# Strassen pairs of a two-layer mixer: weight sums, evacuations and attention spread over fixed steps

## The chip, the cores and the metric

The kernel runs on one core of a Trainium2 chip. The metric is the time of one execution on the device in microseconds (us). A core has five engines that run side by side, each with its own in-order queue: TensorE (PE, matmuls; its weight loads are listed as PEld), VectorE (DVE), ScalarE (ACT), GpSimd (POOL) and SyncE (SP, which here only issues DMAs). They wait for one another and for DMAs through semaphores. An instruction that waits holds up everything behind it on its engine. DMAs are moved by 16 DMA engines; SP and POOL each have a queue to them.

## The reference, cut to what matters

Two layers over a sequence of 1024 rows of 1024 numbers in float32:

```
h = rmsnorm(x, norm_g[l]) * (1 + scale) + shift        # scale, shift, gate from c
p = h @ w_in[l]                                         # 1024 x 1024 by 1024 x 9224
mq, mk, mv, mo, mz, mi, mf, rq, rk, rv, rz = split_cols(p)
y_m = sigmoid(mo) * layernorm(mlstm(silu(conv(mq, mk)), mv, mi, mf)) * silu(mz)     # 4 heads of 256
y_r = layernorm(retention(rotary(rq, rk), rv)) * silu(rz)                           # 4 heads of 256
x = x + gate * (concat(y_m, y_r) @ w_out[l])
```

A final rmsnorm follows. The mLSTM and retention cells are chunkwise attention with a carried state.

## The kernel before, in words

All matrix products are in float32 by three passes: an operand is split into a high part (rounded to fp32r) and a low part (the rest), and `mm3` (L153 to L156) adds high x high, high x low and low x high. A split is a ScalarE cast for the high part and a subtraction on POOL or VectorE for the low part (`split_to`, L758 to L760).

The input projection is the bulk. Two column blocks of weights and the two halves of the sequence form a 2 x 2 block problem, done with seven products in place of eight (a Strassen form, `ORDER` L598). The seven right sides (F, `build_forms` L570) are sums of blocks of the normalised input, made once a layer. The seven left sides are sums of four weight blocks, made anew for each pair by `weight_forms` (L601). Blocks of weights come as 128 x 512 tiles of 256 KB. For one set of seven, `weight_forms` loads three raw tiles on SP's queue (L607), lets POOL issue three accumulating DMAs onto them (L623, L632, L633), makes one sum on VectorE (L627), splits five tiles, and gets the other two sides without a raw tile (`loaded`, L615): POOL's DMA brings the tile straight into the high part (L617), ScalarE writes its negative into the low part (L618), and an accumulating DMA adds the tile again (L619).

`pair_units` (L662) runs the seven products of a pair, twelve wide matmuls each, and yields after each. It evacuates after a product: products 0, 2 and 3 are copied out by ScalarE (L674), since the same bank is accumulated further by a later product, and others are combined by VectorE and handed to `done`, which runs the whole chain for that quarter at once: the gate (L542, L547), convolution and SiLU (`conv_silu` L762), or rotary (`rot_done` L834), and then the split and the stores to DRAM (`spill` L809). `vpair_units` (L690) does the same for the values of two heads, with narrow matmuls, two halves to a step; its copies are L720 and its stores L693.

A layer's order is written by hand in `plan` (L1450): z pairs, q and k pairs of each head, v pairs of two heads, and a pairs (z and o together): 30 jobs, 26 pairs of seven steps and 4 v pairs of fourteen, 238 steps. `Feeder` (L649) makes the left sides in the order of use, at most five ahead (AHEAD = 4), from five high, five low and five raw buffers. `run_units` calls `tick` (L133) after each step; `tick` advances the generators that were launched: `attention` of a head (L862) four ticks after its k pair, the condition rows (`ada_rows` L275), the gate chain, the rotary tables. A head's attention loads q, k and v from DRAM, computes scores, values and state updates for four chunks, and normalises (`normalise` L1027; its root is POOL's L1043 or L1047, its scaling ScalarE's L1051, the transposed store L1060).

PE's order is the program's. The order of the other engines is made by the framework's scheduler from the program's order and a simple model of times; instructions inside `tc.high_priority()` (the evacuations) come earlier. Of the output projection (`OutLoads` L1099, `out_units` L1129) and the startup list (L1352) the change touches little.

Of the kernel before, what the change touches and what calls it, by code (L numbers as in the profile page):

```python
# [19 lines left out]
P = 128  # L20
# [16 lines left out]
NB = 61  # L37
NACC = 6
NTH = 4
NW = 5  # L40
NRAW = 5
AHEAD = 4
# [47 lines left out]
def tile_hybrid_trunk(ctx, tc, x, xt, c, positions, w_ada, b_ada, norm_g, w_in, w_blk, w_val, conv_w, conv_b,  # L90
# [38 lines left out]
    def launch(gen, delay=0):  # L129
        uid[0] += 1  # L130
        pending.append([clock[0] + delay, uid[0], gen])

    def tick():  # L133
        clock[0] += 1
        while True:
            due = [p for p in pending if p[0] <= clock[0]]
            if not due:
                return
            p = min(due, key=lambda q: (q[0], q[1]))
            try:  # L140
                p[0] = clock[0] + next(p[2])
            except StopIteration:
                pending.remove(p)

# [8 lines left out]
    def mm3(o, lt, rt, start, stop, more=False):  # L153
# [29 lines left out]
           for l in range(DEPTH)]  # L183
    mdr = [dpool.tile([NH, T], F32, name=f"mdr{l}") for l in range(DEPTH)]
# [90 lines left out]
    def ada_rows(l, c0, accs):  # L275
        acc = wt("acc", 512, NACC)
        accs.append(acc)
        prev = None
        for k in range(KT + 1):
            raw = None  # L280
            if k < KT:
                raw = wt("acc", 512, NACC)
                Q.dma_start(raw, w_ada[l, k * P:(k + 1) * P, c0:c0 + 512])
            if k == 1:
                V.tensor_scalar(acc, prev, cact[:, 0:1], None, ALU.mult)
            elif k > 1:
                V.scalar_tensor_tensor(acc, prev, cact[:, k - 1:k], acc, ALU.mult, ALU.add)
            prev = raw
            yield 2

    def ada_columns_later(l):
        for half in range(2):
            accs = []
            for which in range(2):
                yield from ada_rows(l, which * D + half * 512, accs)
            yield 2
            pt = ps_a()
            for which in range(2):
                for i in range(4):
                    PE.matmul(pt[:, which * 4 + i:which * 4 + i + 1], accs[which][:, i * P:(i + 1) * P], ones,  # L300
                              start=True, stop=True)
            finish_gsh(l, half * 4, 4, pt[:, 0:4], pt[:, 4:8])
            yield 1

    def gate_rows(l, res):
        for half in range(2):
            accs = []
            yield from ada_rows(l, 2 * D + half * 512, accs)
            brow = wt("th", 512, NTH)
# [5 lines left out]
            a2 = (wt("wH", 512, NW, F32R), wt("wL", 512, NW, F32R))  # L315
# [5 lines left out]
            g = bt()  # L321
            V.tensor_copy(g, pt)
            res.append(g)
# [38 lines left out]
    def load_w_raw(l, c0):  # L362
        for p in range(2):
            raw = wt("raw", 512, NRAW)
            Q.dma_start(raw, w_block(l, c0, p))
            yield raw

    def split_w(raw, eng=G, tiles=None):
        wH, wL = tiles or (wt("wH", 512, NW, F32R), wt("wL", 512, NW, F32R))
        split_to((wH, wL), raw, eng)  # L370
        return [(wH[:, a * P:(a + 1) * P], wL[:, a * P:(a + 1) * P]) for a in range(4)]

    def third(pair, p):
        return [t[:, p * 512:(p + 1) * 512] for t in pair]

    def load_w(l, c0):
        res = []
        for raw in load_w_raw(l, c0):
            res += split_w(raw)
        return res  # L380
# [16 lines left out]
    def rotary_tables():  # L397
        c1, c2, c3 = two_pi_split()
        t0, t1 = wt("q", 1024, 2), wt("kc", 1024, 1)
        ang, turn, tmp, rnd = (t0[:, i * CH:(i + 1) * CH] for i in range(4))  # L400
        a1, pos = (t1[:, i * CH:(i + 1) * CH] for i in range(2))
        a2 = ang
        for n in range(4):
            i, cs = n // 2, slice((n % 2) * CH, (n % 2 + 1) * CH)
            Q.dma_start(pos.bitcast(I32), positions[0:1, n * CH:(n + 1) * CH].to_broadcast([P, CH]))
            yield 2
            V.tensor_copy(ang, pos.bitcast(I32))
            V.tensor_scalar(ang, ang, kc[:, C_FREQ:C_FREQ + 1], None, ALU.mult)
# [4 lines left out]
            V.scalar_tensor_tensor(turn, a2, c2, turn, ALU.mult, ALU.add)  # L413
            for src, cc in ((a1, c2), (a2, c1), (a1, c1)):
# [13 lines left out]
            yield 2  # L428
# [113 lines left out]
    def gate_z(src, g, sign=1.0):  # L542
        th = wt("th", 512, NTH)
# [3 lines left out]
    def gate_o(src, g, store, sign=1.0):  # L547
        th = wt("th", 512, NTH)
# [21 lines left out]
    def build_forms(hT):  # L570
        F = {"11": [hT[k][0] for k in range(4)], "21": [hT[k][0] for k in range(4, 8)],
             "22": [hT[k][1] for k in range(4, 8)], "U1": [], "U2": [], "U3": [], "U4": []}
# [11 lines left out]
        for k in range(4):  # L584
# [8 lines left out]
            u4 = whole(hT[k + 4][0])  # L593
            V.scalar_tensor_tensor(u4, u2, -1.0, u4, ALU.mult, ALU.subtract)
            keep("U4", u4)
        return F
# [4 lines left out]
    def weight_forms(blk, first):  # L601
        def tiles():
            return wt("wH", 512, NW, F32R), wt("wL", 512, NW, F32R)

        def raw(src):
            t = wt("raw", 512, NRAW)
            Q.dma_start(t, src)  # L607
            return t

        def split(r, eng):  # L610
            w = tiles()
            split_to(w, r, eng)
            return w

        def loaded(src):  # L615
            w = tiles()
            G.dma_start(w[0], src)  # L617
            A.activation(w[1], f(w[0]), AF.Copy, scale=-1.0)  # L618
            G.dma_start(w[1], src, accum_op=ALU.add)  # L619
            return w  # L620

        a, s1, s3 = raw(blk[0][0]), raw(blk[1][0]), raw(blk[0][0])
        G.dma_start(s1, blk[1][1], accum_op=ALU.add)  # L623
        if first == "21":
            yield loaded(blk[0][1])
        w = split(a, G)
        V.tensor_tensor(a, a, s1, ALU.add)  # L627
        yield w
        if first == "11":
            yield loaded(blk[0][1])  # L630
        w = split(a, V)
        G.dma_start(a, blk[0][1], accum_op=ALU.add)  # L632
        G.dma_start(s3, blk[1][0], accum_op=ALU.add)  # L633
        yield w
        yield split(s1, G)
        yield split(s3, V)
        yield split(a, G)
        yield loaded(blk[1][1])

    def pair_forms(l, cols2):  # L640
        for w in weight_forms([[w_block(l, c, kh) for kh in range(2)] for c in cols2], "11"):
            yield [(w[0][:, k * P:(k + 1) * P], w[1][:, k * P:(k + 1) * P]) for k in range(4)]

    def vpair_forms(l, heads):
        gens = [weight_forms([[w_val[l, h, kh * 2 + kp] for kh in range(2)] for h in heads], "21") for kp in range(2)]
        for ws in zip(*gens):
            yield [(w[0][:, a * HD:(a + 1) * HD], w[1][:, a * HD:(a + 1) * HD]) for w in ws for a in range(2)]

    class Feeder:  # L649
        def __init__(self, gens):  # L650
            self.gens, self.ready = gens, []
            self.forms = (w for g in gens for w in g())

        def take(self):
            while len(self.ready) <= AHEAD:
                w = next(self.forms, None)
                if w is None:
                    break
# [895 lines left out]
```

## Time and profile before

| what | us |
|---|---|
| median of 2 runs (2924.39 to 2930.87) | 2927.63 |
| the profiled execution | 2911.5 |
| its span, first to last instruction | 2909.8 |
| PE busy in the span | 2279.8 |
| VectorE / ScalarE / POOL busy | 1677.8 / 1142.9 / 1151.3 |
| the longest wait of PE in total, for the copies of L674 | 326.0 |

Busy time of PE is the sum of matmuls that overlap, so a share of 78% does not mean that 22% is left; the spacing of their starts tells. A row of groups gives line, engine, operation, tiles written and read, count, then busy time and mean duration in ns, then the idle time of the engine before them with what ended it. The granted clock is that of PE: 1.00 is full speed.

### The profile page before, as it was taken

The page shows a single profiled execution, that of the slowest core. Times are in us where ns is not written, and L with a number is a line of the kernel's source. Part 1 is how long each engine was busy: PE and PEld are TensorE (multiplying, and loading weights), DVE is VectorE, ACT ScalarE, POOL GpSimd, SP SyncE. Part 2 cuts the span into 40 slices and gives each one's busy share as a digit, 9 for nine tenths or more (in the row PEclk, how much of TensorE's full clock was granted, in tenths as well). Part 3 has the DMA queues.
Part 4 walks back from the last instruction along what each step waited for, and adds up shares of the span by engine and source line. Part 5 has one row for each costly group of instructions (what it writes and reads, how often), then busy time and mean ns, then how long its engine had stood idle before and what let it go on. Part 6 is the DMA issues. An engine that isn't in the chain of part 4 may idle for free. (4 is left out here: it accounts for less than half of the span.)

```text
span 2909.8 us, 35824 instructions
## 1 busy us (share of the span) xinstructions
PE 2279.8 (78%) x11483; PEld 1931.8 (66%) x11483; DVE 1677.8 (58%) x3073; ACT 1142.9 (39%) x2091; POOL 1151.3 (40%) x1174
## 2 busy tenths in 40 slices
PE   4878787768777767689998788788777776777998
PEld 3668666657565755577776677667766575666777
DVE  4875365655655556656638556456455556574744
ACT  4523233233434344444354333333344434353433
POOL 0533454444434343422266344255343434343123
PEclk7978898888898888799998898889888888898999
DMA  6277787878777877768542787688777787776766
GB/s 212 52 169 199 180 222 199 228 215 240 203 208 186 225 205 186 196 172 275 199 141 62 184 223 210 175 231 230 211 205 184 190 223 184 193 203 171 237 209 170
DMA packets 532553, 567.91 MB, mean 195 GB/s; under 512 B 196466, under 2 KB 347770, under 8 KB 532364
## 3 DMA queue, kind: packets, MB, share of 16 engines
q1 hardware_dynamic: 463676, 440.55, 48.3%
q0 software_dynamic: 68544, 124.81, 24.0%
q8 instruction: 90, 1.47, 0.2%
q14 instruction: 99, 0.81, 0.1%
q10 hardware_dynamic: 144, 0.26, 0.0%
HBM read 409.20 MB, written 156.27 MB: 194 GB/s over the span
## 5 line engine op out<-in xcount | busy, mean ns | idle before, releaser
L154 PE MATMUL pp<-b,wH 128*128 128x512 f32 x1616 | 681.6, 422 | 338.1 <-ACT acc L674 326.0
L156 PE MATMUL pp<-b,wL 128*128 128x512 f32 x1616 | 664.8, 411 | 13.3 <-DMA wL<-in_w_blk_dram 8.0
L155 PE MATMUL pp<-b,wH 128*128 128x512 f32 x1616 | 668.0, 413 | 4.3 <-DVE b L1120 4.3
L154 PEld LDWEIGHTS pp<-b,wH 128*128 128x128 f32 x1616 | 327.1, 202 | 431.2 <-ACT acc L674 351.2
L760 POOL TENSOR_TENSOR wL<-raw,wH 128x512 fp32r<-128x512 f32 x276 | 392.0, 1433 | 405.4 <-ACT wH L759 332.2
L759 ACT CAST wH<-raw 128x512 fp32r<-128x512 f32 x476 | 289.7, 616 | 372.0 <-PE pp L155 129.8
L156 PEld LDWEIGHTS pp<-b,wL 128*128 128x128 f32 x1616 | 326.3, 202 | 90.2 <-DMA wL<-in_w_blk_dram 9.3
L155 PE MATMUL pp<-wL,b 128*128 128x256 f32 (+1 forms) x1024 | 325.2, 318 | 64.5 <-DMA wL<-in_w_val_dram 57.7
L155 PEld LDWEIGHTS pp<-b,wH 128*128 128x128 f32 x1616 | 328.5, 203 | 70.1 <-DVE b L1120 6.5
L154 PE MATMUL pp<-wH,b 128*128 128x256 f32 (+1 forms) x1024 | 325.7, 318 | 55.4 <-ACT acc L720 24.5
L156 PE MATMUL pp<-wH,b 128*128 128x256 f32 (+1 forms) x1024 | 321.8, 314 | 0.2
L155 PEld LDWEIGHTS pp<-wL,b 128*128 128x128 f32 x1024 | 215.3, 210 | 74.3 <-DMA wL<-in_w_val_dram 61.0
L154 PEld LDWEIGHTS pp<-wH,b 128*128 128x128 f32 x1024 | 215.0, 210 | 66.6 <-ACT acc L720 25.8
L618 ACT ACTIVATE wL<-wH 128x512 fp32r<-128x512 f32 x136 | 85.7, 630 | 430.2 <-DMA wH<-in_w_blk_dram 288.8
L760 POOL TENSOR_TENSOR acc<-acc,acc 128x512 fp32r<-128x512 f32 x128 | 179.7, 1420 | 156.4 <-ACT acc L759 126.0
L619 POOL DMA_DIRECT2D wL<-in_w_blk_dram x104 | 92.0, 884 | 343.1 <-ACT wL L618 260.4
L760 DVE TENSOR_TENSOR wL<-raw,wH 128x512 fp32r<-128x512 f32 x200 | 156.7, 785 | 111.6 <-ACT wH L759 111.1
L156 PEld LDWEIGHTS pp<-wH,b 128*128 128x128 f32 x1024 | 214.9, 210 | 7.3 <-DVE b L1120 2.4
L771 DVE SCALAR_TENSOR_TENSOR acc<-pp,cols,acc 128x511 f32<-128x511 f32 (+2 forms) x192 | 142.4, 742 | 33.4 <-ACT acc L766 32.1
L627 DVE TENSOR_TENSOR raw<-raw,raw 128x512 f32<-128x512 f32 x68 | 54.8, 807 | 147.7 <-POOL wL L760 104.2
L759 ACT CAST acc<-acc 128x512 fp32r<-128x512 f32 x128 | 78.4, 617 | 130.7 <-DVE acc L848 48.3
L760 POOL TENSOR_TENSOR sL<-th,sH 128x384 fp32r<-128x384 f32 (+1 forms) x64 | 62.3, 973 | 108.9 <-ACT sH L759 87.8
(342 smaller groups left out, 4393.1 us busy)
## 6 DMA issues: line engine op xcount, KB each, us to landing
raw<-in_w_blk_dram SPq DMA_DIRECT2D x171, 256.0 KB
raw<-in_w_blk_dram POOLq DMA_DIRECT2D x156, 256.0 KB, 5.3
vdr<-acc SPq DMA_DIRECT2D x128, 256.0 KB
ring<-vdr SPq DMA_DIRECT2D x64, 512.0 KB
qdr<-acc SPq DMA_DIRECT2D x128, 256.0 KB
q<-qdr SPq DMA_DIRECT2D x64, 512.0 KB
kfr<-acc SPq DMA_DIRECT2D x128, 256.0 KB
kc<-kfr SPq DMA_DIRECT2D x64, 512.0 KB
```

The source lines that it names most:

```text
L154: PE.matmul(o, lt[0], rt[0], start=start, stop=False, skip_group_check=more)
L155: PE.matmul(o, lt[0], rt[1], start=False, stop=False, skip_group_check=more)
L156: PE.matmul(o, lt[1], rt[0], start=False, stop=stop, skip_group_check=more)
L618: A.activation(w[1], f(w[0]), AF.Copy, scale=-1.0)
L619: G.dma_start(w[1], src, accum_op=ALU.add)
L627: V.tensor_tensor(a, a, s1, ALU.add)
L759: A.copy(dst[0], src)
L760: eng.tensor_tensor(dst[1], src, f(dst[0]), ALU.subtract)
L771: V.scalar_tensor_tensor(acc[:, d:], pt[:, 0:HALF - d], wcol, acc[:, d:], ALU.mult, ALU.add)
```

## The change

The weight tiles. Raw tiles and low parts share one ring of 13 buffers (R, 128 x 512); high parts keep five. `Feeder` is now a list of events at fixed steps: each load, sum, high part and low part of a set has its lead before the step that uses it, and `step` emits what is due. All seven loads are plain and on SP's queue; the sums S1, S2, S4 and S3 are accumulating DMAs on POOL's queue, of which S2 += S1 and S4 += S2 read a tile in SBUF. `POOL_LOW` says which low parts POOL makes; VectorE makes the other four.

```
+    NAMES = ("a11", "a12", "S2", "S1", "S3", "S4", "a22")
+    VNAMES = ("a12", "a11", "S2", "S1", "S3", "S4", "a22")
+    POOL_LOW = ("a12", "S3", "a22")
...
+    def ring_load(src):
+        r = wt("R", 512, NR)
+        Q.dma_start(r, src)
+        return r
+
+    def high(r, h=None):
+        h = wt("wH", 512, NW, F32R) if h is None else h
+        A.copy(h, r)
+        return h
+
+    def low(h, r, eng=G):
+        lo = wt("R", 512, NR, F32R)
+        eng.tensor_tensor(lo, r, f(h), ALU.subtract)
+        return lo
...
+        def quad(self, names, blk, t0, u):
+            r, h = {}, {}
+            at = {n: t0 + u * i for i, n in enumerate(names)}
+            a11, a12, a21, a22 = blk[0][0], blk[0][1], blk[1][0], blk[1][1]
...
+            def add(n, src):
+                G.dma_start(r[n], r[src] if isinstance(src, str) else src, accum_op=ALU.add)
...
+            T2 = at["S2"]
+            ev(T2 - 10, load, "S1", a21)
+            ev(T2 - 8, load, "S2", a11)
+            ev(T2 - 8, add, "S1", a22)
+            ev(T2 - 6, load, "S4", a12)
+            ev(T2 - 6, add, "S2", "S1")
+            ev(T2 - 4, add, "S4", "S2")
+            T4 = at["S3"]
+            ev(T4 - 7, load, "S3", a21)
+            ev(T4 - 5, add, "S3", a11)
+            for n, src in (("a11", a11), ("a12", a12), ("a22", a22)):
+                ev(at[n] - 7 + u, load, n, src)
+            for n in names:
+                ev(at[n] - 4 + u, hi, n)
+                ev(at[n] - 2, lo, n, G if n in POOL_LOW else V)
+            return r, h
```

The evacuations. The chains of `done` become generators that are launched and give out one link a step: the convolution (scaling, three shifted sums, tanh, product, transposed copy and split, stores), the gates, the rotary parts, and the stores of the values.

```
+    def conv_chain(l, hg, which, m, half, pt, halo):
...
+        yield 1
         for d in range(1, 4):
...
+        yield 1
+        th = wt("acc", 512, NACC)
         A.activation(th, acc, AF.Tanh, scale=0.5)
+        yield 1
         V.scalar_tensor_tensor(acc, th, 1.0, acc, ALU.add, ALU.mult)
-        return acc
+        yield 1
+        yield from spill(acc, l, hg, which, m, half)
...
+        A.copy(hi, src)
+        G.tensor_tensor(lo, src, f(hi), ALU.subtract)
+        yield 1
+        for o, t in late:
+            Q.dma_start(o, t)
         Q.dma_start(dst[m], f(hi))
         Q.dma_start(dst[2 + m], src)
```

Attention follows a table of 43 steps, one entry a step; `scores` and `update` are generators of three links, the sums of the values and `normalise` are launched a step later, and loading and splitting of the transposed k are apart ("t" and "s"). A lock lets the next head begin when the one before has reached step 23; a head's attention is launched 6 steps after its k pair, in place of 4.

```
+    TABLE = ("q0 k0 v0 d0 d1 t0", "", "", "m0", "s0 S0", "k1", "m1 q1", "v1", "V001", "S1 t1", "U01",
+             "k2 q2 d2", "s1 v2", "V10 U2 m2", "S2", "k3 d3", "V11 U3", "t2 q3", "s2 v3", "", "V20 U4 m3", "S3", "",
+             "V21 U5", "", "", "", "V30", "V31", "")
+    RELEASE = 23
...
+        while busy[0]:
+            yield 1
+        busy[0] = True
+        for n, step in enumerate(TABLE):
+            if n == RELEASE:
+                busy[0] = False
+            for what in step.split():
+                run(what)
+            yield 1
```

Around these: the sums of the right sides (`build_forms`) are a generator that gives out one k a step, the last set four steps later, launched before the gate products; the plan of jobs is reordered, with v pairs and z pairs moved; the condition rows of the next layer (or the gate rows of the last, which now go through DRAM) start at step 30 (or 2) of a layer, in place of after certain k pairs; the tags acc (6) and th (4) become acc alone with 11 buffers; the b pool has 59 in place of 61; sH and sL have one buffer each in place of two.

```
-    plan = ("v45 v67 v01 q4 k4 z4 q5 k5 z5 q6 k6 z6 q7 k7 z7 q0 k0 a10 a11 q1 k1 v23 q2 k2 a20 q3 k3 a21 a30 a31",
-            "v45 q4 k4 z4 q5 k5 v67 q6 k6 z5 z6 q7 k7 v01 q0 k0 z7 a10 q1 k1 v23 q2 k2 a11 a20 q3 k3 a21 a30 a31")[l]
+    plan = ("v45 v67 z4 q4 k4 z5 q5 k5 v01 q6 k6 q7 z6 k7 q0 a10 k0 v23 q1 k1 a11 q2 k2 q3 a20 k3 z7 a21 a30 a31",
+            "v45 q4 k4 z4 q5 k5 v67 q6 k6 z5 q7 k7 v01 q0 k0 z6 a10 q1 k1 v23 q2 k2 a11 q3 k3 a20 z7 a21 a30 a31")[l]
```

Last, the order of all engines but PE is made from a fuller model of times, in place of the simple one:

```
-    with tile.TileContext(nc) as tc:
+    with tile.TileContext(nc, schedule_with_timeline_sim=True) as tc:
```

More of the change, by code (lines that the diff above doesn't have):

```diff
@@ L360, in w_block, with split_w, tiles4 @@
         return w_blk[l, (c0 - 8 * (c0 > OFF_I)) // P, p]
[L362 to L374, printed above, removed]
+    def ring_load(src):
[10 more added lines that the diff above has]
+        return lo
+    def split_w(r, eng=G, h=None):
+        h = high(r, h)
+        return tiles4(h, low(h, r, eng))
+    def tiles4(h, r):
+        return [(h[:, a * P:(a + 1) * P], r[:, a * P:(a + 1) * P]) for a in range(4)]
     def load_w(l, c0):
         res = []
[L378 to L379 removed]
+        for r in [ring_load(w_block(l, c0, p)) for p in range(2)]:
+            res += split_w(r)
         return res
@@ L704, in vpair_units @@
         for n, (b, form) in enumerate(VORDER):
-            w = feed.take()
             for part in range(2):
+                feed.step()
+                if part == 0:
+                    w = feed.take()
                 bank, keep = banks[part], keeps[part]
@@ L830, in done @@
             if m:
-                one(1, 1, late[0])
+                one(1, 1, late[0], 1)
         return done
```

433 lines of the change are left out of this document (225 added, 208 removed).

## The prediction

> **What bounds the kernel now.** I read the page first, then the busy time by stage, the waits of TensorE, one of those waits in the timelines, and the groups of instructions. The page gives the span and the DMA queues:
>
> ```profile
> span 2909.8 us, 35824 instructions
> ...
> q1 hardware_dynamic: 463676, 440.55, 48.3%
> q0 software_dynamic: 68544, 124.81, 24.0%
> ```
>
> The stages, each row with its length, then busy time (and count) of PE, PEld, DVE, ACT, POOL, then granted clock, DMA share, GB/s. The first and third are the Strassen products of the two layers, the second is most of the first layer's output projection:
>
> ```profile
> 119.30:1312.00 1192.70, 895.43 (x4670) 767.66 (x4669) 713.72 (x1354) 439.42 (x819) 483.92 (x509) 0.87 0.75 198
> 1312.00:1500.00 188.00, 180.53 (x798) 147.46 (x797) 95.01 (x153) 83.91 (x140) 75.26 (x58) 0.99 0.65 217
> 1561.00:2686.00 1125.00, 862.25 (x4504) 745.20 (x4503) 644.40 (x1176) 429.82 (x800) 479.53 (x504) 0.87 0.76 197
> ```
>
> The output projection is as full as PE gets. The two product stages, 1192.7 + 1125.0 = 2317.7 us, are not, at a clock of 0.87. Busy time hides how far off they are, because matmuls overlap. The timeline of PE gives the true spacing and one of the waits:
>
> ```profile
> 2440.39 0.28 PE L156 MATMUL pa<-ring,b 128*128 128x258 f32 x1
> 2440.51 0.40 PE L154 MATMUL pp<-b,wH 128*128 128x512 f32 x1
> ...
> 2443.01 0.40 PE L156 MATMUL pp<-b,wL 128*128 128x512 f32 x1
> ...
> 2455.03 0.80 PE L154 MATMUL pp<-b,wH 128*128 128x512 f32 x1 [11.15 <-ACT acc L674]
> ```
>
> The twelve matmuls of one product start in 2.50 us over eleven steps: 0.227 us each, 2.73 us a product; a narrow one (256 or 258 columns) takes 0.12, as the first two rows show. By the code both layers have 52 pairs of 84 wide matmuls (4368) and 8 v pairs of 336 narrow ones (2688); the windows count 9174 in all, so some 2118 belong to attention and the gates. At full pace that is 4368 x 0.227 + 4806 x 0.12 = 1568 us. The stages take 2317.7, so 750 us are waiting and slow clock. PE's longest waits (total, times, longest):
>
> ```profile
> PE pp L154 <- ACT acc L674: 326.0, 54, 17.7
> PE pp L155 <- DMA wL<-in_w_val_dram: 57.7, 15, 8.1
> ...
> PE pp L154 <- ACT acc L720: 24.5, 5, 13.3
> ```
>
> Nearly half of the 750 is one thing: PE cannot go on with a bank until ScalarE has copied it out (L674; L720 is the same in the v pairs). ScalarE is not busy (439 of 1193 us); its queue in the very wait above shows why the copy is late:
>
> ```profile
> 2451.68 0.63 ACT L775 ACTIVATE th<-acc 128x512 f32<-128x512 f32 x1 [2.87 <-DVE va L1041]
> 2452.89 1.09 ACT L1051 ACTIVATE n<-nd,nmu,rsd 128x256 f32<-128x256 f32 x2 [0.58 <-DVE nmu L1049]
> 2453.89 0.60 ACT L759 CAST acc<-acc 128x512 fp32r<-128x512 f32 x1
> 2454.40 0.58 ACT L674 COPY acc<-pp 128x512 f32<-128x512 f32 x1
> ```
>
> A copy of 0.58 us stands behind the tanh of the convolution, which waits for VectorE, and behind the attention's scaling. Elsewhere it stands behind weight splits that wait for a load just issued (L618) or for a buffer that PE still reads (L759):
>
> ```profile
> ACT wL L618 <- DMA wH<-in_w_blk_dram: 288.8, 87, 8.1
> ACT wH L759 <- PE pp L155: 129.8, 73, 5.5
> ```
>
> **The change part by part.** (1) *Clock.* The wide matmuls have a longer mean in the product stages than in the output projection:
>
> ```profile
> L154 PE MATMUL pp<-b,wH 128*128 128x512 f32 x1616 | 681.6, 422 | 338.1 <-ACT acc L674 326.0 <-ACT b L1119 7.1 <-ACT wH L759 4.0
> L155 PE MATMUL pp<-b,wH 128*128 128x512 f32 x1616 | 668.0, 413 | 4.3 <-DVE b L1120 4.3
> ...
> L154 PE MATMUL pa<-b,wH 128*128 128x512 f32 x128 | 49.8, 389 | 0.0
> ```
>
> (422 + 413) / 2 - 389 = 28 ns by the 4848 matmuls of the three groups of 1616 is 138 us. It stands mostly behind long waits: the first matmul after the wait above takes 0.80 us in place of 0.39.
>
> (2) *Evacuations and attention, one product a step.* Each chain (conv, gate, rotary, store, scores, state) now gives out one link per product, so that ScalarE's next link depends on VectorE work emitted one product, 2.7 us or more, earlier. Nothing is added to PE. This and part 3 aim at 326.0 + 24.5 = 350 us of waits and, in proportion to 350 of some 612 us of waits in these stages (750 - 138), at 79 us of slow clock: at most 429 us. Attention now also holds a lock for 23 steps a head; the last head would start at step 220 (layer 0) or 211 of 238, and its first half is wanted some 14 products into the output projection, about 30 steps later, against the 20 that it needs. I cost it at nothing; its cover is the output projection, which takes heads 4 to 7 first. The output loads, the norm and the startup list keep their instructions: nothing, 15 us either way for the new order.
>
> (3) *Weights.* Per block of seven products (52 + 16 = 68 blocks: a v pair has two):
>
> ```profile
> L760 DVE TENSOR_TENSOR wL<-raw,wH 128x512 fp32r<-128x512 f32 x200 | 156.7, 785 | 111.6 <-ACT wH L759 111.1
> ...
> L619 POOL DMA_DIRECT2D wL<-in_w_blk_dram x104 | 92.0, 884 | 343.1 <-ACT wL L618 260.4 <-ACT cf L969 36.2 <-ACT b L806 9.4
> ...
> L627 DVE TENSOR_TENSOR raw<-raw,raw 128x512 f32<-128x512 f32 x68 | 54.8, 807 | 147.7 <-POOL wL L760 104.2
> ```
>
> VectorE: two low parts and one sum become four low parts, 68 x (4 x 785 - 2 x 785 - 807) ns = +52 us. POOL: three low parts stay; seven DMA issues become four, 204 fewer at 0.884 us, -180 us. ScalarE: seven casts stay. VectorE would then be 713.7 + 644.4 + 52 = 1410 us of the stages' new length, 0.70 at 2000 us. SP: three loads become seven, 272 more issues, without waits for what was made in the same step; its cover is that SP does nothing else, and without it the loads would be late, which the DMA bound below takes in.
>
> DMA: before, ten transfers of 256 KB per block, seven of them on POOL's queue; after, eleven: seven loads on SP's, four accumulations on POOL's. Price on SP's queue: 48.3% of 2909.8 = 1405 us for 440.55 MB, 0.836 us per 256 KB. On POOL's: 698 us for 124.81 MB (476 transfers), 1.47 us on the mean; if its 136 plain ones cost 0.836, its 340 accumulating ones cost 1.72. After: 272 x (1.47 to 1.72) + 272 x 0.836 more on SP's queue - 698 = -71 to -3 us. Two of the four now read SBUF instead of HBM, which no row shows; between the 1.47 of the mean and twice 1.72 as the far end (+234 us on 136), I take 1.72 as the nearest, being an accumulation of the same size, and the middle of the above: -40.
>
> On the Trainium skill's page "DMA: Bandwidth & Descriptors" (section Issuing engines are not separate DMA queues) transfers of all queues run on the same 16 engines, so a move from POOL's queue to SP's would save no transfer time; by it the term is 0 and the result 40 / 0.855 = 47 us later.
>
> (4) *What is late next: DMA.* The stages hold 0.75 x 1192.7 + 0.76 x 1125.0 = 1750 us of full DMA, more than PE's 1568. So DMA sets the pace once the waits go. The best that the kernel held for long is two slices of the second layer:
>
> ```profile
> 1891.40:2036.90 145.50, 123.61 (x570) 101.39 (x570) 81.93 (x149) 52.30 (x99) 76.40 (x80) 0.93 0.88 230
> ```
>
> With 1710 us of DMA: at 0.88, 1943 us; at 0.80 (little over now), 2137; at 0.93, 1839. The whole stage will hardly hold its best, as jobs differ; I take 0.855: 2000 us, 318 less than now, three quarters of the 429. With 238 steps a layer a step goes from 2317.7 / 476 = 4.87 to 4.20 us.
>
> The sum: the profiled execution took 2911.5 us (span 2909.8); 2911.5 - 318 = 2593. The median shown, 2927.63, is 0.55% above, so 2593 x 1.0055 = 2608, rounded 2610.
>
> **The rivals.** *PE sets the pace.* DMA reaches 0.95 and more; PE stays 10% off its floor: 1568 / 0.9 = 1742, less 576: 2350. For it: DMA demand would be evened out by fixed leads. Against it: only 0.88 was held, and by one window.
>
> *The copies stay late.* Convolution chains now hold their acc buffers over five products, eleven buffers stand for the ten of acc and th, and VectorE at 0.70 runs in bursts (the timeline's copy waited for it). Then about a third of the 429 goes, 143: 2780, from 2700 to 2860. For it: the wait shown begins with VectorE, to which 52 us are added.
>
> *The change does not do what it says:* the order made from a model puts other waits where these were: 2920, from 2850 to 2985. For it: the waits of ScalarE and VectorE in the profile are many and short, and any of them can grow. Against it: the largest, L618's, loses its cause, a load issued just before it.
>
> *Slower: the chained sums land late.* The second sum reads the first, the third the second, two products apart each, and the issue stands in POOL's queue until the one before has landed; behind it wait the low parts and the attention's root (L1043), behind these ScalarE and PE. POOL's accumulating transfers land (last column, us) after:
>
> ```profile
> raw<-in_w_blk_dram POOLq DMA_DIRECT2D x156, 256.0 KB, 5.3
> ```
>
> A step is then half a landing: it decides from 2 x 4.87 = 9.7 us on. At 11 us a step is 5.5 us and the stages 2618: +300, 3230. For it: a fuller DMA lands later. Against it: 5.3 us at a share of 0.75 is little over half of 9.7.
>
> On the same page's rules (Rules for kernel authors) a transfer that reads what another wrote must wait for that one's semaphore, so the chain cannot overlap itself. Its fit of about 2.0 us plus bytes over 436 GB/s (section Anatomy of one DMA) makes 2.6 us an estimate for 256 KB, with which this rival would fall away; the trace has 5.3, which decides, and the rival keeps its chance.
>
> **How the numbers follow.** DMA pace 0.54 (own range 2440 to 2750), PE pace 0.08 (half of it below 2340), late copies 0.18, no change 0.07 (half of it above 2870), slower 0.13. The range 2340 to 2870 leaves out 0.04 + 0.03 + 0.13 = 0.20. About 2% is what a measurement of this kernel can tell from no change: faster (under 2869) 0.54 + 0.08 + 0.18 = 0.80; within 2% 0.07; slower 0.13. The predicted time is that of the DMA pace.
>
> **What would show it.** Right: PE's wait for ACT acc (the copies) falls from 326 us to under 100; the clock in the product stages rises from 0.87 above 0.93; their DMA share rises above 0.82; no ScalarE wait for a weight load stays over 50 us. DVE busy grows by some 50 us and POOL's shrinks by some 180. PE pace is right if matmuls in these stages stand under 10% off 1568 us. Wrong: waits of POOL's issues or of ScalarE's casts for the sums at the head of the list (slower), or the copies there again, behind VectorE (late copies).

## The result, and the profile after

The kernel after takes 2450.56 us (median of two runs, 2449.08 to 2452.03) where the kernel before takes 2927.63: a ratio of 0.837, with an interval of 0.8325 to 0.8416. The prediction was 2610. The profiled execution took 2452.03 us, its span is 2450.3.

The first view is the page of after: busy time of each engine, then the two queues that count (packets, MB, share of 16 DMA engines), then landing times of POOL's sums.

```profile
PE 2187.5 (89%) x11483; PEld 1865.7 (76%) x11483; DVE 1777.1 (73%) x3165; ACT 1130.7 (46%) x2093; POOL 1055.0 (43%) x978
...
q1 hardware_dynamic: 503420, 512.92, 66.1%
q0 software_dynamic: 39168, 71.32, 17.4%
...
R<-R POOLq DMA_DIRECT2D x136, 256.0 KB, 5.5
```

Before, PE was busy 2279.8 us and idle for 630; now 2187.5 and 263. Busy time counts matmuls that overlap once, not as a sum: their own durations add up to 4155.9 us before and 4051.6 after. So of the 459 us of span, 367 are idle time of PE and 92 are time in which PE was busy. Its groups of matmuls, with mean ns after the busy time, show the second part: 422 and 413 ns have become 406 and 402.

```profile
L155 PE MATMUL pp<-b,wH 128*128 128x512 f32 x1616 | 656.7, 406 | 92.3 <-ACT acc L716 53.0
L156 PE MATMUL pp<-b,wH 128*128 128x512 f32 x1616 | 649.6, 402 | 10.5 <-DVE b L1214 10.5
```

Next, the stages of after (length; busy time and count of PE, PEld, DVE, ACT, POOL; granted clock, DMA share, GB/s). The first and third are the product stages.

```profile
106.00:1055.00 949.00, 845.08 (x4653) 735.29 (x4652) 767.23 (x1397) 437.40 (x825) 430.23 (x410) 0.95 0.92 259
1055.00:1321.00 266.00, 244.19 (x1064) 195.35 (x1063) 127.48 (x202) 116.88 (x188) 112.09 (x86) 0.96 0.53 168
1321.00:2239.00 918.00, 833.72 (x4636) 727.10 (x4634) 713.08 (x1274) 433.81 (x828) 435.47 (x415) 0.96 0.91 257
```

The whole gain is in the product stages. Cut by the same ends they were 1192.7 and 1150.0 us before; the prediction's cut of the second ended 25 us earlier, and this is the whole row of before:

```profile
1561.00:2711.00 1150.00, 882.35 (x4610) 762.22 (x4608) 660.12 (x1212) 441.41 (x823) 484.04 (x511) 0.87 0.76 196
```

Those two stages got 476 us shorter and startup 13, while the two output projections got 17 and 12 longer. In the first stage the clock rose from 0.87 to 0.95 and the DMA share from 0.75 to 0.92.

Last, the waits of PE and of ScalarE in after (total, times, longest). The copies are now L716, and L766 in the v pairs.

```profile
PE pp L155 <- ACT acc L716: 53.0, 26, 4.7
...
PE pp L155 <- ACT acc L766: 17.6, 6, 6.2
```
```profile
ACT wH L381 <- PE pp L156: 190.8, 125, 3.7
...
ACT wH L381 <- DMA R<-in_w_out_dram: 84.6, 35, 7.1
...
ACT wH L381 <- DMA R<-in_w_blk_dram: 53.4, 23, 6.6
```

350 us of waits for copies have become 71, the longest of them 6.2 us in place of 17.7. ScalarE's longest wait is now for a buffer that PE still reads, which means that there it is ahead of PE.

### The profile page after: what moved, and what is told of

It is laid out like the page before. It is cut to its first block, busy times and chain, and to the rows that moved or that the text cites. A ratio compares the mean times of both kernels' runs of the same rounds, so it can differ in the third digit from the quotient of the medians.

```text
span 2450.3 us, 36202 instructions
## 1 busy us (share of the span) xinstructions
PE 2187.5 (89%) x11483; PEld 1865.7 (76%) x11483; DVE 1777.1 (73%) x3165; ACT 1130.7 (46%) x2093; POOL 1055.0 (43%) x978
## 3 DMA queue, kind: packets, MB, share of 16 engines
q1 hardware_dynamic: 503420, 512.92, 66.1%
q0 software_dynamic: 39168, 71.32, 17.4%
## 5 line engine op out<-in xcount | busy, mean ns | idle before, releaser
L157 PE MATMUL pp<-b,R 128*128 128x512 f32 x1616 | 647.1, 400 | 0.0
L381 ACT CAST wH<-R 128x512 fp32r<-128x512 f32 x616 | 377.3, 618 | 505.1 <-PE pp L156 190.8
L386 POOL TENSOR_TENSOR R<-R,wH 128x512 fp32r<-128x512 f32 x276 | 397.7, 1446 | 410.0 <-ACT wH L381 314.1
L386 DVE TENSOR_TENSOR R<-R,wH 128x512 fp32r<-128x512 f32 x340 | 268.5, 791 | 141.5 <-ACT wH L381 136.2
L157 PEld LDWEIGHTS pp<-b,R 128*128 128x128 f32 x1616 | 314.4, 195 | 69.5
L156 PE MATMUL pp<-R,b 128*128 128x256 f32 (+1 forms) x1024 | 316.4, 309 | 11.1 <-DVE R L386 11.0
L661 POOL DMA_DIRECT2D R<-R x136 | 123.0, 912 | 285.5 <-DMA R<-in_w_blk_dram 138.4
L156 PEld LDWEIGHTS pp<-R,b 128*128 128x128 f32 x1024 | 206.9, 202 | 19.8 <-DVE R L386 14.5
L661 POOL DMA_DIRECT2D R<-in_w_blk_dram x104 | 100.7, 968 | 146.1 <-DMA R<-in_w_blk_dram 90.4
L833 DVE SCALAR_TENSOR_TENSOR acc<-pp,cols,acc 128x510 f32<-128x510 f32 (+1 forms) x192 | 140.1, 737 | 2.2 <-ACT acc L827 1.9
L716 ACT COPY acc<-pp 128x512 f32<-128x512 f32 x156 | 90.5, 581 | 8.8 <-PE pp L157 3.3
```

The source lines that it names most:

```text
L156: PE.matmul(o, lt[0], rt[1], start=False, stop=False, skip_group_check=more)
L157: PE.matmul(o, lt[1], rt[0], start=False, stop=stop, skip_group_check=more)
L381: A.copy(h, r)
L386: eng.tensor_tensor(lo, r, f(h), ALU.subtract)
L661: G.dma_start(r[n], r[src] if isinstance(src, str) else src, accum_op=ALU.add)
L716: A.copy(keep[n], bank["Z" if n == 3 else "X"])
```

## The experiments

**Which part did it.** The change is taken here in three parts: the weight path with its plain loads, the spacing of chains and attention, and the order from the fuller model. What else was changed (the plan of jobs, the right sides given out one k a step, the start of the condition rows, the bigger acc pool) goes with the spacing in these runs; none takes it alone. Theory A: the copies wait in ScalarE's queue, and spacing and weights together clear it. Theory B: the order does it. Theory C: the weights do. Four kernels were made from the pieces.

Only the order taken back:

```
-    with tile.TileContext(nc, schedule_with_timeline_sim=True) as tc:
+    with tile.TileContext(nc) as tc:
```

> The changed kernel with the scheduler's simple model of times again; program unchanged. Theory A (ScalarE's queue: the copies were late because links of the chains and weight splits that waited stood ahead of them, and spacing the links removes that in any reasonable order): 2450 to 2560 us, PE's wait for the copies stays under 120 us. Theory B (the order from the fuller model is what pays): 2750 us or more, the copies' wait back over 250 us. Theory C (the weights: plain loads with leads pay): as A, about 2450 to 2550.

Measured: 2740.35 us, ratio 0.9363 (0.9327 to 0.9399). The order is worth 290 us on the changed program. No theory had that: B's time is only 10 us off, but its reason is not there, since PE's waits for copies stay at 68 us, as A has it.

The kernel before with the order alone (the same line the other way):

> The kernel before, with the order of all engines but PE made by the fuller model, and nothing else. Theory A and theory C: 2860 to 2980 us, within 2% of 2928, the copies' wait over 250 us. Theory B: 2450 to 2600.

Measured: 2818.95 us, ratio 0.9632 (0.9552 to 0.9711). So the order alone is 109 us; all three theories miss.

The kernel before with the new weight path alone (the `Feeder` of events, `quad`, `ring_load`, `high` and `low` of after in place of `weight_forms`; one buffer each for sH and sL, as after):

```
-NB = 61
+NB = 60
...
-NRAW = 5
-AHEAD = 4
+NR = 13
...
+            feed.step()
             w = feed.take()
```

> The kernel before with the new weights alone: one ring (13 buffers), loads, sums, high and low parts at the fixed leads; chains, attention, plan and scheduler's model as before (one big buffer fewer, one scores buffer fewer). Theory A: a part, 2700 to 2800 us, since casts no longer wait for loads just issued, but the copies still stand behind whole chains (their wait 150 to 250 us). Theory B: 2850 or more. Theory C: most of it, 2450 to 2580.

Measured: 2892.59 us, ratio 0.9883 (0.9815 to 0.9952): 35 us, about 1%. C falls, A's 2700 to 2800 is missed too, and B's 2850 or more holds.

The kernel after with the weight path of before (the same edit the other way, but sH and sL keep one buffer):

> The changed kernel with the weights of before (three raw loads, POOL's loads into the high part, five raw, high and low buffers), all else as changed. Theory A: a part again, 2600 to 2750 us, ScalarE's wait for the load of wH back at some 300 us. Theory B: 2450 to 2550. Theory C: 2800 or more.

Measured: 2641.52 us, ratio 0.9025 (0.8983 to 0.9067). A's time holds and B falls, but A has missed in the other runs, and the waits say what is missing. The two largest rows of PE's waits in each of these four kernels, in the same sequence (the copies are L716, L674, L698 and L695):

```profile
PE pp L157 <- DVE R L386: 113.3, 40, 8.2
PE pp L155 <- ACT acc L716: 49.2, 28, 5.7
```
```profile
PE pp L154 <- ACT acc L674: 305.4, 43, 14.7
PE pp L155 <- DMA wL<-in_w_val_dram: 59.4, 17, 6.3
```
```profile
PE pp L153 <- ACT acc L698: 277.1, 53, 16.5
PE pp L154 <- DVE R L373: 57.4, 16, 19.8
```
```profile
PE pp L157 <- DMA wL<-in_w_val_dram: 66.3, 16, 7.9
PE pp L156 <- ACT acc L695: 59.6, 29, 7.3
```

Where the chains are given out in bursts (the second and third), the copies are late whatever the weights and the order are. Where they are spaced (the first and fourth), the copies come, and PE waits for weights instead: for low parts (R) that VectorE makes late, or for the accumulating loads onto low tiles (wL). This makes a new theory S: the spacing ends the waits for copies; the new weight path and the fuller order end the waits for weights, but only both together.

**Which spacing.** In e3 every `launch` of an evacuation, gate, convolution or spill chain becomes a call that runs the chain whole; in e4 the same is done to gathering, normalising, scores and update of attention, whose table (it has 30 entries, not 43) stays. In e12 the edits of e1 and e6 are made together, which leaves the spacing, the plan and the other small parts.

```
+    def at_once(gen, *_):
+        for _ in gen:
+            pass
...
-            launch(conv_chain(l, hg, which, m, half, src, halos[m]), delay)
+            at_once(conv_chain(l, hg, which, m, half, src, halos[m]), delay)
```

> The kernel after, but each evacuation, gate, convolution and spill chain is given out whole when its product ends, and not one piece a product; attention stays spaced, and so do weights and order. In the five programs seen so far TensorE's waits for ScalarE's copies (the sum over acc) were 350, 354 and 299 us where nothing was spaced (before, order alone, weights alone) and 68, 80 and 75 us where all was spaced (simple order, all but weights, after). Theory S1, the chains' bursts make the copies late: waits for copies back to 200 us or more, 2620 to 2760 us. Theory S2, the attention pieces do: copies' waits stay below 130 us, 2450 to 2540 us.

Measured: 2672.72 us, ratio 0.9124 (0.9065 to 0.9183). Bursts of the chains cost 222 us.

> The kernel after, but gathering, normalising, scores and update of attention are given out whole; the evacuation chains stay spaced. Theory S1 (the chains' bursts make the copies late): copies' waits below 130 us, 2450 to 2540 us. Theory S2 (the attention pieces do): copies' waits of 200 us or more, 2620 to 2760 us. If both programs land between 2540 and 2620 us, each half of the spacing removes part of it.

Measured: 2477.67 us, ratio 0.8458 (0.8403 to 0.8513). This part of attention's spacing comes to 27 us, little over 1%; S1 holds in both runs.

> The kernel before's weight path and its simple order, with the chains and attention spaced as after. Theory S (spacing alone ends the copies' waits; the plain weights and the fuller order together end the waits for weights): waits for copies below 110 us, waits for weight tiles between 100 and 220 us, 2680 to 2800 us. Rival (spacing acts only with the new weight path or with the fuller order): copies' waits above 250 us, 2860 to 2940 us.

Measured: 2847.42 us, ratio 0.9720 (0.9674 to 0.9766): between the two forecasts. The waits of PE in e3, and then in e12:

```profile
PE pp L159 <- ACT acc L720: 256.7, 43, 14.7
...
PE pp L159 <- ACT acc L770: 26.2, 10, 6.2
```
```profile
PE pp L156 <- ACT acc L695: 102.4, 36, 7.3
PE pa L156 <- ACT b L851: 77.3, 20, 12.5
PE pp L157 <- DMA wL<-in_w_val_dram: 58.1, 10, 8.5
PE pp L158 <- DMA wL<-in_w_blk_dram: 45.0, 20, 7.0
PE pp L156 <- ACT acc L743: 37.2, 7, 10.1
```

Alone, the spacing takes 350 us of copies' waits to 143, not below 110; and the split of the transposed k (L851) becomes a wait of 77 us. The mechanism stands in e3's queue of ScalarE, in the last 9.3 of the 14.69 us in which PE waits for one copy (start, length, line; in brackets the idle time before it and its cause):

```profile
1041.22 0.63 ACT L842 ACTIVATE acc<-acc 128x512 f32<-128x512 f32 x1 [4.86 <-issue]
1042.61 0.62 ACT L887 CAST acc<-acc 128x512 fp32r<-128x512 f32 x1 [0.76 <-DVE acc L844]
1043.13 0.77 ACT L831 ACTIVATE acc<-pp,cols 128x512 f32<-128x512 f32 x1
1048.00 0.63 ACT L842 ACTIVATE acc<-acc 128x512 f32<-128x512 f32 x1 [4.10 <-DVE acc L839]
1049.39 0.62 ACT L887 CAST acc<-acc 128x512 fp32r<-128x512 f32 x1 [0.76 <-DVE acc L844]
1049.91 0.58 ACT L720 COPY acc<-pp 128x512 f32<-128x512 f32 x1
```

Links of two convolution chains stand ahead of a copy of 0.58 us: scaling (L831; the first chain's ran at 1034.56), then the tanh (L842), which comes 4.10 us late in the second chain for want of VectorE's shifted sums and 4.86 us in the first (put down to issue), then the cast of the spill (L887). ScalarE works 3.9 us of these 9.3. A queue in order makes the copy wait for VectorE, though it needs nothing of it. VectorE's queue shows what delayed the first chain: a low part of the weights, which ran for 3.59 us between two of its shifted sums (L837), while POOL ran tensor operations from 1036.35 to 1039.13:

```profile
1036.10 3.59 DVE L390 TENSOR_TENSOR R<-R,wH 128x512 fp32r<-128x512 f32 x1
1039.61 1.52 DVE L837 SCALAR_TENSOR_TENSOR acc<-pp,cols,acc 128x510 f32<-128x510 f32 x2
```

In e1 the same thing happens one engine further on. VectorE's queue ahead of a low part (L386) for which PE waits 6.74 us:

```profile
960.67 0.47 DVE L1019 SCALAR_TENSOR_TENSOR acc<-pa,eul,dm 128x256 f32<-128x256 f32 x1
961.06 0.73 DVE L833 SCALAR_TENSOR_TENSOR acc<-pp,cols,acc 128x511 f32<-128x511 f32 x1
961.72 0.41 DVE L1021 TENSOR_TENSOR acc<-acc 128x256 f32<-128x256 f32 x1
962.05 2.05 DVE L833 SCALAR_TENSOR_TENSOR acc<-pp,cols,acc 128x510 f32<-128x510 f32 x3
964.02 0.68 DVE L386 TENSOR_TENSOR R<-R,wH 128x512 fp32r<-128x512 f32 x1
```

The low part is not blocked but ordered behind convolution and attention work: ScalarE's last weight cast before it had ended at 955.27, and VectorE was busy without a break from 956.47 on. The simple model puts it there; under the fuller one PE's waits for VectorE's low parts are 11 us in place of 144. Of the 290 us, PE's waits are 202 and its longer busy time 84.

With e3 for bursts, new weights and the fuller order (attention stays spaced in it, and the plan is the new one), this makes all eight combinations. Waits are sums of all of PE's rows, for copies (ScalarE's acc) and for weight tiles (R, wH, wL), in us:

| chains | weights | order | time | waits for copies | waits for weights |
|---|---|---|---|---|---|
| bursts | old | simple (before) | 2928 | 350 | 87 |
| bursts | new | simple (e5) | 2893 | 299 | 189 |
| bursts | old | fuller (e2) | 2819 | 354 | 81 |
| bursts | new | fuller (e3) | 2673 | 283 | 20 |
| spaced | old | simple (e12) | 2847 | 143 | 131 |
| spaced | new | simple (e1) | 2740 | 68 | 225 |
| spaced | old | fuller (e6) | 2642 | 80 | 139 |
| spaced | new | fuller (after) | 2451 | 75 | 20 |

S holds in its second half by every row: waits for weights fall to 20 us in the two rows with new weights and the fuller order, and in no other. In its first half it holds but for e12, where spacing alone goes only to 143. The parts done alone sum to 224 us (80 + 35 + 109), together they give 477: a product starts when the latest of its supplies is there, so a part that mends one alone mostly uncovers the other. The sizes are those of the spacing with what goes with it; for the chains alone e3 gives 222.

**What sets the pace now.** The prediction said that DMA would. Theory D is that; theory P says TensorE with its clock and its many short waits. The first trial adds one plain transfer a set:

```
+            def more():
+                extra[0] += 1
+                Q.dma_start(spare[extra[0] % 4], a11)
+
+            ev(T2 - 3, more)
```

> The kernel after with one more plain transfer of 256 KB for each of the 68 weight sets, from the weights in memory to a spare place in memory that nobody reads. A plain 256 KB takes 0.76 to 0.84 us of all 16 DMA engines in these traces, so DMA work grows by about 54 us, most of it in the two product stages, which hold 1708 us of DMA work in 1867 us. Theory D (transfers now set the pace at a share of 0.915): 54/0.915 = 59 us more, 2495 to 2525 us. Rival P (TensorE with its clock and the remaining waits sets the pace, and the share of 0.91 is only what its work comes to): 2445 to 2470 us, share up to 0.94.

Measured: 2470.72 us, ratio 0.8434 (0.8402 to 0.8466), between the two. The trace shows that it missed its place, as the next expectation tells: startup to the first v pair took 116.7 us in place of 106, and the second layer's stage did not grow. The second trial ties the transfer to the high part of S3 (`Q.dma_start(spare[extra[0] % 4], f(h[n]))` at one step before its use).

> The run with 68 more transfers (2470.72 us) put them elsewhere than meant: 53 of them left in the first 116 us and all 68 before 133 us, since nothing held them back, and there the startup grew by 11 us. Here each set's extra 256 KB is written from the high part of S3, made one or two products before, so that it can't leave early: one transfer per set, about 47 us of DMA work in the product stages, which hold 1702 us in 1867 us. Theory D (transfers set the stages' pace at 0.915): 52 us more, 2495 to 2515 us. Theory P (TensorE with its clock and the short waits sets it; transfers only where a stretch is full, as 384 to 667 us at 1.00): 2452 to 2478 us, share in the stages 0.93 to 0.95.

Measured: 2465.35 us, ratio 0.8443 (0.8413 to 0.8472). DMA work on SP's queue grew by 44 us (66.1% of 2450.3 to 67.5% of 2464.9) and the time by 15 (2464.12 to 2466.58 against 2449.08 to 2452.03). Between the same products, after first and then e13 (startup to first v pair, to the second, to the output projection, then the second layer):

```profile
106.00:367.80 261.80, 222.23 (x1263) 197.67 (x1262) 213.90 (x347) 98.32 (x173) 118.28 (x97) 0.92 0.81 229
367.80:651.20 283.40, 259.06 (x1447) 225.97 (x1446) 228.71 (x415) 123.77 (x233) 137.20 (x131) 0.96 1.00 290
651.20:1103.00 451.80, 409.81 (x2175) 350.42 (x2175) 358.37 (x710) 237.98 (x460) 182.97 (x189) 0.96 0.89 252
1321.60:2239.40 917.80, 833.12 (x4634) 726.59 (x4632) 712.88 (x1275) 433.56 (x828) 434.87 (x415) 0.96 0.91 257
```
```profile
105.00:372.70 267.70, 224.60 (x1266) 199.82 (x1265) 217.05 (x348) 99.03 (x174) 115.76 (x98) 0.92 0.82 233
372.70:667.50 294.80, 262.65 (x1448) 229.29 (x1447) 233.94 (x415) 123.47 (x232) 136.44 (x131) 0.94 0.98 289
667.50:1119.40 451.90, 410.71 (x2174) 352.41 (x2174) 355.02 (x710) 238.09 (x460) 183.87 (x189) 0.96 0.91 260
1336.80:2253.10 916.30, 830.72 (x4633) 725.17 (x4631) 711.86 (x1275) 434.02 (x828) 430.81 (x415) 0.96 0.93 267
```

The stretch that held a share of 1.00 grew by 11.4 us and the one before it by 5.9. The other two, at 0.89 and 0.91, took more transfers at no cost, as P has it. One trace each leaves some play: e7, whose last extra transfer was issued at 134.4 us, has the first stretch 4.9 us longer than after, the second within 1 and the others up to 4 off. So D can hold in one stretch of 283 us at most, and it is not shown there either: its DMA work grew by some 5 us (1.00 x 283.4 to 0.98 x 294.8), and in e14 below, without one transfer more, the same stretch is 7.5 us longer.

The third trial goes the other way. It leaves the sums of weights out (the accumulating transfers are not issued, so S1 to S4 stay unsummed):

```
-                G.dma_start(r[n], r[src] if isinstance(src, str) else src, accum_op=ALU.add)
+                return
```

> The kernel after without the four accumulating transfers of each set: S1 to S4 keep what was loaded first, so the sums of weights are not formed; all else stays. It takes 272 transfers and 407 us of DMA work from the product stages (share 0.915 to about 0.70), and 272 issues from POOL. Theory D: TensorE is next, whose matmuls come to 1584 us in the stages at the full clock's spacing; 1584/0.92 = 1722 instead of 1867: 2280 to 2340 us. Theory P (TensorE with its clock and the waits already sets the pace): 2380 to 2445 us, copies' waits still above 50 us. Rival W (chained sums are what ScalarE's casts and POOL's low parts wait for): POOL's wait for R from weights (228.9 us) and ScalarE's for R (138 us) go, and the time falls below 2380 through TensorE's waits of 254 us falling under 150.

Measured: 2357.16 us, ratio 0.8072 (0.8026 to 0.8118): below P's range and above D's. Its product stages:

```profile
106.00:1008.00 902.00, 832.35 (x4656) 728.68 (x4655) 732.09 (x1396) 437.78 (x823) 321.54 (x280) 0.96 0.75 235
...
1271.00:2140.00 869.00, 815.62 (x4633) 716.64 (x4632) 687.95 (x1273) 432.95 (x827) 333.60 (x285) 0.98 0.74 232
```

With some 388 us of DMA work less, the stages got 96 us shorter. Theory D gave them 145, down to 1722, where TensorE would set the pace. W's time is met, but not by its reason alone: PE's waits in all fell from 254 to 186 us, not under 150, and 55 of them are still for copies. The stretch that held a share of 1.00 got 12 us shorter, 4%, and the other three 5% each, so it was not held back more than they were. The run takes away the transfers, 272 issues of POOL and the waits for sums together, so how much of the 96 us is due to the DMA engines stays open.

**The chain of sums.** The slower rival said that sums which land late would hold up the queues. Here the links stand one product apart in place of two:

```
-            ev(T2 - 10, load, "S1", a21)
-            ev(T2 - 8, load, "S2", a11)
-            ev(T2 - 8, add, "S1", a22)
+            ev(T2 - 7, load, "S1", a21)
+            ev(T2 - 7, load, "S2", a11)
+            ev(T2 - 6, add, "S1", a22)
...
-            ev(T2 - 6, add, "S2", "S1")
+            ev(T2 - 5, add, "S2", "S1")
```

> The kernel after with the links of the chain S1, S2, S4 one product (3.9 us) apart instead of two; the sums land 5.5 to 6.6 us after their issue (median 5.5). The prediction's slower rival: a link waits at POOL for the one before, 2 to 3 us three times a set, and low parts and ScalarE behind it, up to 68 x 3 x 2.5 = 510 us if nothing hides it: 2700 to 2960 us; half hidden 2600 to 2700. Theory slack: POOL, busy 43%, has the room, the chain is still complete before its casts: 2445 to 2500 us.

Measured: 2508.12 us, ratio 0.8589 (0.8555 to 0.8623): 58 us slower than after, between the two forecasts. ScalarE's wait for these sums, 10.4 us in after, is now its largest but one:

```profile
ACT wH L381 <- PE pp L156: 167.2, 103, 6.9
ACT wH L381 <- DMA R<-R: 144.6, 49, 10.0
```

So the mechanism exists, but its price is a ninth of the 510 us that it was costed at for this run. The wait shows more at ScalarE's casts than at POOL's issues, whose waits for such sums rise from 40.5 to 69.2 us. PE's waits rise from 254 to 295 us in many small rows, of which those for ScalarE's weight casts stay at 7. The plain loads of S1 and S2 also go out later here, and the run does not separate the two.

**A version aimed at what is left.** Two edits: the low part of S2 goes to POOL (`POOL_LOW = ("a12", "S2", "S3", "a22")`), and `loads.stage(2)` loads two pieces ahead of each output projection.

> The kernel after with two small edits that aim at waits still in its trace. The low part of S2 goes from VectorE (0.81 busy in the first product stage) to POOL (0.45): 68 low parts, 53 us less on VectorE, 96 us more on POOL; TensorE waits 82 us in all for VectorE's acc and b. And each output projection starts with two pieces loaded ahead; TensorE waits 11 + 9 us there for the gated activations (b L1213) and 10 for b L1214. If VectorE is what is late where TensorE waits for it: 2405 to 2440 us, waits for VectorE under 60 us. Rival: POOL, in whose queue the low parts wait behind links that wait for landings (229 us), delivers S2 late, or the same TensorE time is lost elsewhere: 2445 to 2480 us, with waits for R up.

Measured over five rounds: 2466.29 us, ratio 0.8437 (0.8414 to 0.8461). No gain over after; the rival holds. VectorE lost 68 low parts and was busy 1794.4 us, not less than the 1777.1 of after: its low parts took 46.8 us less, and other instructions more, sums of two tiles in SBUF (L287) 19.0 us of it. The rows of after show a reason. They give min, median and max ns of a product of two tiles in SBUF (L840) and of a shifted sum that reads one of its inputs from PSUM (L833):

```profile
L840 DVE SCALAR_TENSOR_TENSOR acc<-acc,acc x64: 645/684/3869, 585.8 to 2119.1; 128x512 f32<-128x512 f32 x64
```
```profile
L833 DVE SCALAR_TENSOR_TENSOR acc<-pp,cols,acc x192: 703/737/750, 578.5 to 2112.8; 128x511 f32<-128x511 f32 x64, 128x510 f32<-128x510 f32 x64, 128x509 f32<-128x509 f32 x64
```

The second hardly varies, the first goes to 5.7 times its median. For the low parts it goes with who began first. Of the 342 low parts of VectorE in the trace of after, 258 have no two-input tensor operation of POOL beside them and a median of 684 ns; 30 began before one of POOL's and have 684 as well (four of them took longer); 46 began while one of POOL's had 0.2 us or more to go, and have 1183. Where only one of POOL's lies beside them (30 of the 46), 22 end 0.54 to 0.56 us after it, as if they had to wait for its end. In e14 the mean of L840 rises from 923 to 1001 ns. That what left VectorE came back as waiting beside POOL fits these numbers, but was not tested by itself. The Trainium skill's page "SBUF — State Buffer" (section Who interferes with whom) says that a VectorE instruction with two SBUF inputs contends with a GpSimd instruction that reads SBUF, and one with a single SBUF input does not; these rows agree. Which of the two edits cost what was not separated.

## Why the prediction was right in sign and short in size

*What bounds the kernel before* was read rightly: the copies' waits went from 350 to 71 us, and e3, by the chains' bursts alone, brings them back to 283, in the way that the quoted queue showed.

*(1) and (2), at most 429 us.* Too low. The copies gave 280 of their 350. The matmuls gave 65 against 79 by the prediction's own measure (its two means stood 28 ns above 389 and now stand 15 above), and 92 by PE's busy time. That measure adds up durations of 0.39 us that start 0.227 apart, so its 138 us were not all time on the span. Beyond these, waits that the sum did not touch went too: 67 us for weights, 25 for ScalarE's b tiles, 24 for loads of k (each the sum of PE's rows of that kind); waits for VectorE's acc and b tiles grew, from 40 to 82. The limit took in the largest wait only.

*"Nothing, 15 us either way for the new order."* This is the step that failed by the most: 290 us on the changed program (e1), 109 alone (e2). The order was costed from the parts of the program that keep their instructions; but the order also decides where a low part stands in VectorE's queue.

*(3) Weights.* VectorE +99 us against +52: the low parts and the sum went from 211.5 to 268.5, +57; the rest lies in other instructions, such as sums of two tiles in SBUF (L287, from 824 to 948 ns), while those that read PSUM did not lengthen (L771, now L833, 742 to 737). POOL -96 against -180: the count of issues is right (476 to 272), but their time went from 408 to 252 us, -156, since 104 of those that went are L617's at 0.669 us where 0.884 was taken and the ones that stay cost 0.91 to 0.97; and POOL's other instructions took 60 us more. DMA -58 (2103.8 to 2046.0) against -40, within its bounds. Sums read from SBUF are not dearer: 17.4% of 2450.3 us by 272 is 1.57 us each, where 1.72 was taken.

*(4) DMA sets the pace.* The DMA work of the stages was forecast at 1710 us and is 0.92 x 949 + 0.91 x 918 = 1708. The term that was mis-sized is the share: 0.915 was held, not 0.855, so a step takes 3.92 us, not 4.20, and the stages lost 476 us, not 318 (25 of the difference come from the prediction's earlier cut). The reason given for it can be right for one stretch of the first layer at most (e13, e9). So two errors met, a limit taken too low and a bound that mostly does not bind, and that the time still fell inside the DMA pace's own range, 2440 to 2750, is in part luck.

*The rivals.* Late copies is what e3 makes, at 2673. PE's pace, forecast at 2350, is not reached: the stages stand 19% off the 1568 us of full pace; e9, without sums, reaches 2357 with 13%. The slower rival needed a landing of two steps, 9.7 us at the pace of before and 7.8 at that of after; sums land after 5.5 to 6.3, and e10, which does put the links under a landing apart, costs 58 us. Half of its sign is there: POOL's issues wait 228.9 us for R from the weights (plain loads or the first sums), its second largest wait, but PE's waits for POOL's low parts are 1.6 us. Of the signs, copies under 100 us, a clock above 0.93 and a share above 0.82 came as said; "no ScalarE wait for a weight load over 50 us" did not: 84.6 and 53.4 are left, but PE's waits for ScalarE's weight casts are 7 us, so PE hardly pays for them.

## What to carry to other kernels

A long wait for a short instruction is read in the queue of the engine that runs it: what stands ahead of it and what that waits for; here spacing the chains that another engine feeds took PE's waits for copies from 283 to 75 us (e3 and after). When several supplies are late by turns, the worth of one part measured alone says little: 224 us apart were 477 together, so try parts in pairs before dropping one. A high DMA share is not yet a bound: add some transfers that can't run ahead, take some away, and see which stretches move.

## What the runs showed of the hardware

An accumulating transfer of 256 KB takes 1.57 us of all 16 DMA engines on the mean here, a plain one on SP's queue about 0.83 (66.1% of 2450.3 us for 512.92 MB). The accumulating one lands after 5.5 us with an SBUF source and after 6.3 with the weights in memory as source (medians). The DMA engines held a share of 1.00 for 283 us with PE at a clock of 0.96. VectorE's low parts, with two SBUF inputs, take 684 ns alone or when they begin first, and 1183 (median of 46) when they begin while a tensor operation of POOL runs; the shifted sums that read PSUM stay at 737. And the granted clock goes with the idle time: over these kernels PE's waits of 621, 457, 388, 254 and 186 us go with a granted clock of 0.888, 0.918, 0.925, 0.952 and 0.963 (before, e1, e6, after, e9), and with 367 us of idle time 92 us of PE's busy time went as well.
